# A hybrid decoder layer on one core: MLA's query norm applied in the softmax, its squares on ScalarE, and another order of the projections

## The chip, the cores and the metric

The kernel runs on one core of a Trainium2 chip. The metric is the device time of one execution in microseconds. Of a kernel, one execution is profiled; its trace gives start and length of each instruction on TensorE (PE; its weight loads are PEld), the vector engine (DVE), ScalarE (ACT), GpSimd (POOL) and the DMA queues (SP issues them).

## The reference

One decoder layer over 256 tokens, width 2048, float32. Half an FFN, then two groups of heads side by side, then half an FFN again:

```
x = x + 0.5 * swiglu(rms_norm(x, ffn1_norm), ...)           # d_ff 5632
proj = rms_norm(x, mix_norm) @ w_in
(q_a, k_cmp, v_cmp, k_sel, v_sel, k_win, v_win, g_a, c_q, c_kv, k_rope) = split(proj)
o_a = nsa_mixer(...)      # 8 sparse heads of 128: compressed, selected and window keys, gated
o_b = mla_mixer(...)      # 8 heads, below
x = x + concat(rms_norm(o_a), rms_norm(o_b)) @ w_out
x = x + 0.5 * swiglu(rms_norm(x, ffn2_norm), ...)

def mla_mixer(c_q, c_kv, k_rope, ...):
    q = (rms_norm(c_q, q_a_gain) @ w_uq).reshape(B, S, 8, 192)
    kv = (rms_norm(c_kv, kv_a_gain) @ w_ukv).reshape(B, S, 8, 256)
    k_nope, v = kv[..., :128], kv[..., 128:]
    k = concatenate([k_nope, k_rope of each head], -1)
    q = rms_norm(q, q_gain); k = rms_norm(k, k_gain)          # over 192
    q, k: the last 64 of 192 rotated by position (rope)
    s = q @ k^T * 192 ** -0.5, causal;  p = softmax(s);  o = p @ v
```

## The kernel before

Every weight is read once, as float32, and split into two parts that TensorE takes at its full rate: ScalarE casts `w_hi`, the vector engine subtracts to give `w_lo`. A product is then three matmuls (`mm3`). Weights come through three `raw` buffers on SP's queue in the order in which `weights` lists them; five split pairs may be ahead (`SPLIT`). In the middle part only as many as `SOON` allows are split at once; others wait until ScalarE and the vector engine have nothing more urgent.

All instructions are written out by a planner when the kernel is built. `go` keeps a clock per engine from rough costs. At each step it lets a finished split go on, then a side task (a generator that yields the condition it waits for), and only then the next piece of the dense stream of matmuls. The order that comes out is fixed: on the chip each engine runs its list in order and waits where an operand is late.

The middle part (`mix`) has this dense stream: the compressed keys, then tokens' projections by `TOKENS` ("0" and "1": four sparse queries each, "g": gates and MLA's query latent, 408 columns, "c": MLA's key latent, 320 columns), then by `MERGE` four up projections of queries (`q0` to `q3`, 384 columns, two heads each), four of keys and values (`k0` to `k3`, 512 columns), and the output projection in 16 pieces (`p0` to `p7` read the sparse heads, so wait for all of them, `p8` to `p15` the MLA heads).

Beside it run the heads as side tasks. A sparse head (`nsa_head`): scores into banks `ps_s`; on the vector engine bias added and maximum taken (`p_e`, `p_m`); exponential with sums on ScalarE (`p_z`); scaling on the vector engine; two "flips", transposes on TensorE into `ps_t`, each copied to `p_t` by ScalarE; the weighting of values into `ps_t`; `gather` evicts it (ScalarE `mha` and the square `sq`, vector engine `mha` and `oss`). An MLA head (`mla_head`) has one such softmax. `ps_t` has two banks in turn, which all transposes share.

An up projection's result is copied by ScalarE to a `wait` tile (four of them). For a query pair `up_q_rest` then squares it on the vector engine (`dot`, result `mss`), takes 1/sqrt (`rsqrt`: four steps on the vector engine, ten on GpSimd, scratch tiles `nw_v`, `nw_w`, `nw_t`), multiplies the 192 columns of each head by it (`mrs`), rotates the last 64 (`rope`: gain, cosine, sine, result `qr`), and turns it by transposes into `mla`. `up_k_rest` does the like for keys. The task's second number in `spawn` is its rank: rank 2 and 3 also wait until the vector engine's clock is near.

Of the kernel before, what the change touches and what calls it, by code (L numbers as in the profile page):

```python
# [7 lines left out]
F32 = mybir.dt.float32  # L8
# [28 lines left out]
TOKENS = "0g1c"  # L37
WEAVE = "abababab"

MERGE = [(m[0], int(m[1:])) for m in "q0 q1 q2 q3 k0 k1 p0 k2 p1 k3 p2 p3 p4 p5 p6 p7 p8 p9 p10 p11 p12 p13 p14 p15".split()]  # L40
PACE = 3.0

LAG, SOON = 1.0, 2
# [121 lines left out]
class _Layer:  # L165
# [637 lines left out]
    def mix(self, h, ssq, after):  # L803
# [4 lines left out]
        with self.tc.tile_pool(name="mx", bufs=1) as mx, ExitStack() as early, ExitStack() as lately:  # L808
# [19 lines left out]

            pos = const("pos", [P, 2, 32], 1)
            okc = const("okc", [P, 2])  # L830
            rot = const("rot", [P, 2, 2, 64])
            rgain = const("rgain", [P, 2, 64])
# [81 lines left out]
            self.spawn(clear())  # L914

# [188 lines left out]
            def latent_kv(p):  # L1104
# [47 lines left out]
            mla = {}  # L1152
# [37 lines left out]
            def up_q_end(i, p):  # L1190
                arrays()
                ss = brief([P, 2, 2], "mss", bufs=8)
                rs = brief([P, 2, 2], "mrs", bufs=8)
# [5 lines left out]
                self.spawn(up_q_rest(i, n, qs, ss, rs), 2)  # L1199
# [187 lines left out]
            def mla_head(hd):  # L1387
                i, j = divmod(hd, 2)
                H = hd + 8
                yield self.at(f"qT{i}", f"kT{i}", f"s{H - 1}", f"f{H - 2}")  # L1390
# [10 lines left out]
                z = brief([P, 2, 2], "p_z", bufs=2)  # L1401
# [193 lines left out]
```

## Time and profile before

| | us |
|---|---|
| three executions, median | 1822.61 (1820.01 to 1823.04) |
| the profiled execution | 1822.96 |
| its span, first to last instruction | 1821.2 |
| TensorE busy | 1800.5 |
| vector engine busy | 1457.4 |
| ScalarE busy | 992.9 |
| GpSimd busy | 45.3 |

The span is what the trace covers; 1.8 us lie around it. Busy times of engines overlap. TensorE's matmuls are pipelined, and a busy TensorE at half clock counts as busy: the granted clock has to be read beside it. The middle part lies between some 740 and 1115 us of the span.

### The profile page before, as it was taken

Reading aid. Unit: us, or ns where it says so; the run is one execution under the profiler, and the core shown is the slowest. Engines: PE = TensorE matmul, PEld = TensorE weight load, DVE = VectorE, ACT = ScalarE, POOL = GpSimd, SP = SyncE. Lnnn points to the kernel's source line nnn. Section 1 sums busy time; section 2 is a strip of 40 time slices with the busy share of each in tenths; the row PEclk is TensorE's granted clock in tenths of the full one; section 3 lists DMA queues with packets and bytes.
Section 4 is the critical chain, followed back from the end, with each engine's and each line's share of the span. In section 5 each row is a group of like instructions: output and inputs, shape, how many; then the busy total and the mean of one; then the engine's idle time right before and its main releaser. Section 6 shows DMA issues by size and latency. Waiting matters only on the chain.

```text
span 1821.2 us, 30455 instructions
## 1 busy us (share of the span) xinstructions
PE 1800.5 (99%) x12187; PEld 1645.0 (90%) x12187; DVE 1457.4 (80%) x2273; ACT 992.9 (55%) x1381; POOL 45.3 (2%) x132
## 2 busy tenths in 40 slices
PE   9999999999999999999998999999999999999999
PEld 8999999999999998888876789999999999999997
DVE  5887878979798896766778766787878989798894
ACT  6565655555555544555564545465655555555542
POOL 0000000000000000001013000000000000000000
PEclk9999999999999999999998999999999999999999
DMA  8555555555555555675233255455555655555554
GB/s 323 181 196 196 195 209 185 209 185 190 204 194 203 190 189 174 219 266 201 93 120 128 93 185 173 175 201 192 189 205 187 209 183 205 188 208 202 191 182 144
DMA packets 55950, 344.30 MB, mean 189 GB/s; under 512 B 6656, under 2 KB 8960, under 8 KB 19200
## 3 DMA queue, kind: packets, MB, share of 16 engines
q1 hardware_dynamic: 55808, 342.36, 54.0%
q8 instruction: 95, 1.56, 0.3%
q14 instruction: 47, 0.39, 0.1%
HBM read 340.24 MB, written 2.10 MB: 188 GB/s over the span
## 4 chain that ended last, share of the span: by engine, by line
PE 94%; DVE 3%; ACT 1%; DMA 1%; issue 1%; POOL 0%; SPq 0%; DVEq 0%; ACTq 0%
PE ps_u L281 47%; PE ps_m L281 19%; PE ps_acc L281 14%; PE ps_g L281 4%; PE ps_l L281 4%; PE ps_s L281 3%; DVE w_lo L141 1%; PE ps_t L281 1%; PE ps_t L296 1%; DMA raw<-in_ffn_first 0%; DVE junk L141 0%; ACT h L141 0%; DVE h L141 0%; DVE wait L141 0%; DMA raw<-in_w_cmp 0%
## 5 line engine op out<-in xcount | busy, mean ns | idle before, releaser
L141 DVE TENSOR_TENSOR w_lo<-raw,w_hi 128x1024 fp32r<-128x1024 f32 (+3 forms) x649 | 767.7, 1199 | 219.8 <-ACT w_hi L141 219.0
L141 ACT CAST w_hi<-raw 128x1024 fp32r<-128x1024 f32 (+3 forms) x649 | 660.7, 1033 | 505.0 <-PE ps_u L281 221.7
L281 PE MATMUL ps_u<-h,w_hi 128*128 128x256 f32 x4864 | 855.2, 279 | 0.0
L281 PEld LDWEIGHTS ps_u<-h,w_hi 128*128 128x128 f32 x4864 | 746.2, 188 | 6.9
L281 PE MATMUL ps_u<-h,w_lo 128*128 128x256 f32 x2432 | 679.2, 279 | 0.0
L281 PEld LDWEIGHTS ps_u<-h,w_lo 128*128 128x128 f32 x2432 | 457.1, 188 | 0.3
L281 PE MATMUL ps_m<-w_hi,act 128*128 128x512 f32 x1008 | 329.0, 396 | 0.0
L141 ACT CAST w_hi<-tsum 128x1024 fp32r<-128x1024 f32 (+1 forms) x144 | 120.6, 838 | 213.4 <-DVE tsum L141 117.9
L281 PEld LDWEIGHTS ps_m<-w_hi,act 128*128 128x128 f32 x1008 | 189.9, 188 | 43.0
L281 PE MATMUL ps_m<-w_lo,act 128*128 128x512 f32 x504 | 199.8, 396 | 0.0
L141 DVE TENSOR_TENSOR w_lo<-tsum,w_hi 128x1024 fp32r<-128x1024 f32 (+1 forms) x144 | 134.6, 953 | 33.8 <-ACT w_hi L141 33.7
L281 PE MATMUL ps_acc<-w_hi,h 128*128 128x512 f32 (+2 forms) x384 | 120.3, 381 | 0.0
L281 PEld LDWEIGHTS ps_m<-w_lo,act 128*128 128x128 f32 x504 | 94.6, 188 | 19.5
L141 DVE TENSOR_TENSOR tsum<-tsum,raw 128x512 f32<-128x512 f32 x144 | 98.5, 684 | 0.0
L281 PE MATMUL ps_l<-w_hi,act 128*128 128x512 f32 x256 | 82.6, 398 | 0.0
L281 PEld LDWEIGHTS ps_acc<-w_hi,h 128*128 128x128 f32 x384 | 71.2, 188 | 12.3 <-issue 1.6
L281 PE MATMUL ps_g<-h,w_hi 128*128 128x256 f32 x448 | 79.0, 280 | 0.2 <-DVE ff_g L141 0.2
L281 PE MATMUL ps_acc<-w_lo,h 128*128 128x512 f32 (+2 forms) x192 | 71.6, 373 | 0.0
L281 PE MATMUL ps_acc<-h,w_hi 128*128 128x256 f32 (+1 forms) x320 | 69.9, 307 | 0.8 <-ACT w_hi L141 0.8
L281 PEld LDWEIGHTS ps_g<-h,w_hi 128*128 128x128 f32 x448 | 68.2, 188 | 0.3 <-issue 0.3
L281 PE MATMUL ps_g<-h,w_lo 128*128 128x256 f32 x224 | 62.4, 279 | 0.0
L281 PEld LDWEIGHTS ps_l<-w_hi,act 128*128 128x128 f32 x256 | 48.2, 188 | 11.3
(244 smaller groups left out, 1702.9 us busy)
## 6 DMA issues: line engine op xcount, KB each, us to landing
raw<-in_ffn_gate SPq DMA_DIRECT2D x83, 1024.0 KB, 4.8
raw<-in_ffn_up SPq DMA_DIRECT2D x83, 1024.0 KB, 4.8
raw<-in_ffn_down SPq DMA_DIRECT2D x72, 1024.0 KB, 4.8
raw<-in_ffn_rest SPq DMA_DIRECT2D x32, 512.0 KB, 3.3
raw<-in_w_out SPq DMA_DIRECT2D x16, 1024.0 KB, 4.8
raw<-in_w_q SPq DMA_DIRECT2D x8, 1024.0 KB, 4.9
raw<-in_ffn_first SPq DMA_DIRECT2D x7, 768.0 KB, 8.0
raw<-in_w_cmp SPq DMA_DIRECT2D x4, 1024.0 KB, 4.8
```

What stands on the lines that cost most here:

```text
L141: r = f(*args, **kw)
L281: self.nc.tensor.matmul(out, l, r, start=start, stop=stop)
L296: self.nc.tensor.transpose(out, src, self.ident if ident is None else ident)
```

## The change

The norm of MLA's queries is no longer multiplied into them. They are rotated and turned as they come from the projection. Their squares are taken afterwards by ScalarE, 1/sqrt of the sums (`mrs`, and `mns` with the sign turned, one more step of GpSimd) is kept per pair in `qn`, and the softmax applies it: the exponential takes it as its scale, and the maximum is multiplied by it (`p_mb`), eight small steps of the vector engine. The keys keep their scaling, but ScalarE takes their squares. The gains of the rotated part are multiplied into cosine and sine once (`rots`), so a rotation has two multiplies where it had three. `rsqrt` gets scratch tiles of its own for queries and keys, two of each. Three settings of the order change as well.

```diff
-TOKENS = "0g1c"
+TOKENS = "0gc1"
-MERGE = [... "q0 q1 q2 q3 k0 k1 p0 k2 p1 k3 p2 p3 p4 p5 p6 p7 p8 ... p15".split()]
+MERGE = [... "q0 k0 q1 k1 q2 k2 q3 k3 p0 p1 p2 p3 p4 p5 p6 p7 p8 ... p15".split()]
-LAG, SOON = 1.0, 2
+LAG, SOON = 1.0, 3
+            def square(out, x, n):
+                junk = sp.tile([P, 512], F32, name="junk", tag="junk")
+                S.activation(junk[:, :n], x, AF.Square, accum_out=out)
...
+            def turning():
+                yield self.fresh(rot, rgain)
+                yield self.at("rbm")
+                for i in range(2):
+                    for m in range(2):
+                        V.tensor_mul(rots[:, i, m], rot[:, m], rgain[:, i][:, None, :].to_broadcast([P, 2, 64]))
+                self.mark("rots", rots)
...
-            def up_q_rest(i, n, qs, ss, rs):
+            def up_q_rest(i, n, qs):
                 yield self.fresh(qs)
-                for tb in range(2):
-                    for j in range(2):
-                        dot(ss[:, tb, j:j + 1], qs[:, tb, j], 192)
-                yield self.fresh(ss)
-                self.rsqrt(rs, ss, "m", 1.0, 192 * EPS)
-                yield self.fresh(rs)
                 if i:
                     yield self.at(f"qT{i - 1}")
                 qr2 = brief([P, 2, 2, 64], "qr2")
-                for tb in range(2):
-                    V.tensor_mul(qs[:, tb], qs[:, tb], rs[:, tb][:, :, None].to_broadcast([P, 2, 192]))
-                self.rope(qr2, qs[:, :, :, P:], rgain[:, 0], rot, brief, 2)
-                yield self.fresh(qs)
+                self.rope(qr2, qs[:, :, :, P:], rots[:, 0], brief, 2)
                 yield self.slot()
                 yield from up_turn(qs, qr2, i, "qT", "qr", G_MQ)
+                for tb in range(2):
+                    yield lambda: S.clk - LAG
+                    for j in range(2):
+                        square(ss[:, tb, j:j + 1], qs[:, tb, j], 192)
                 self.mark(f"left{n}")
+                yield self.fresh(ss)
+                self.rsqrt(rs, ss, f"mq{i % 2}", 1.0, 192 * EPS)
+                G.tensor_scalar(ns, rs, -1.0, None, op0=ALU.mult)
+                qn[i] = rs, ns
...
             def up_k_rest(i, n, ks, ss, rs):
-                        dot(ss[:, tb, j:j + 1], ks[:, tb, j], P)
+                        square(ss[:, tb, j:j + 1], ks[:, tb, j], P)
-                self.rsqrt(rs, ss, "m", 1.0 / 192, EPS)
+                self.rsqrt(rs, ss, f"mk{i % 2}", 1.0 / 192, EPS)
...
             def mla_head(hd):
-                    soft(e, z, m, 0, lo, n, tb, s[:, lo:lo + n], biases[8])
+                    V.tensor_tensor_reduce(out=e[:, lo:lo + n], in0=s[:, lo:lo + n], in1=biases[8][:, lo:lo + n], scale=-1.0,
+                                           scalar=3e38, op0=ALU.add, op1=ALU.min, accum_out=m[:, tb, 0:1])
+                V.tensor_mul(mb, m[:, :, 0], rs[:, :, j])
+                for tb, (lo, n) in enumerate(HALF):
+                    S.activation(e[:, lo:lo + n], e[:, lo:lo + n], AF.Exp, scale=ns[:, tb, j:j + 1], bias=mb[:, tb:tb + 1],
+                                 accum_out=z[:, tb, 0:1])
...
     def rope(...):
-        V.tensor_mul(g, src, gain[:, None, None, :].to_broadcast(sh))
-        V.tensor_mul(c, g, rot[:, 0][:, :, None, :].to_broadcast(sh))
-        V.tensor_mul(g, g, rot[:, 1][:, :, None, :].to_broadcast(sh))
+        V.tensor_mul(out, src, rot[:, 0][:, :, None, :].to_broadcast(sh))
+        V.tensor_mul(g, src, rot[:, 1][:, :, None, :].to_broadcast(sh))
```

The order on the vector engine, where a query pair of before is normed and rotated (`mss`, `mrs`: squares and norms of a pair, `wait`: the pair, `ISA` the squaring with its accumulator read). Before:

```order
L141 TENSOR_SCALAR nw_v<-mss 128x4
L141 TENSOR_SCALAR nw_w<-mss 128x4
L141 TENSOR_SCALAR mrs<-nw_v 128x4
L141 TENSOR_SCALAR mrs<-mrs 128x4
L141 TENSOR_TENSOR wait<-wait,mrs 128x384 x2
L141 TENSOR_TENSOR ro_g<-wait,rgain 128x256
L141 TENSOR_TENSOR ro_c<-ro_g,rot 128x256
L141 TENSOR_TENSOR ro_g<-ro_g,rot 128x256
L141 TENSOR_TENSOR qr_10225<-ro_c,ro_g 128x4x32 x2
L141 SCALAR_TENSOR_TENSOR mha<-ps_t,par,mha 128x256
L141 TENSOR_TENSOR oss_8985<-oss_8985,sq 128x256
L141 ISA junk,mss<-wait 128x192
```

In the changed kernel, the same step of the third query pair, with head 5's eviction and the start of head 7's scaling behind it:

```order
L141 TENSOR_SCALAR nw_v<-mss 128x4
L141 TENSOR_SCALAR nw_w<-mss 128x4
L141 TENSOR_SCALAR mrs<-nw_v 128x4
L141 TENSOR_SCALAR mrs<-mrs 128x4
L141 TENSOR_TENSOR qr_10273<-wait,rots 128x256
L141 TENSOR_TENSOR ro_g<-wait,rots 128x256
L141 TENSOR_TENSOR qr_10273<-qr_10273,ro_g 128x4x32 x2
L141 SCALAR_TENSOR_TENSOR mha<-ps_t,par,mha 128x256
L141 TENSOR_TENSOR oss_8990<-oss_8990,sq 128x256
L141 RECIPROCAL p_z<-p_z 128x4
L141 TENSOR_TENSOR p_z<-p_z,gate 128x4
L141 TENSOR_SCALAR p_e<-p_e,p_z 128x128 x2
```

The pair is only rotated; its square, its scaling and one multiply are gone from this queue, and the four short steps ahead of it belong to another pair's norm.

The order on TensorE around the scores of the last sparse heads (`nsa` holds their queries and keys, `cT` the latents that the up projections read). Before, from head 7's scores to the next flip (`p_e`):

```order
L281 MATMUL ps_s<-nsa 128x256
L281 MATMUL ps_s<-nsa 128x512
L281 MATMUL ps_t<-p_t,nsa 128x256
L281 MATMUL ps_t<-p_t,nsa 128x128
L281 MATMUL ps_t<-p_t,nsa 128x256
L281 MATMUL ps_t<-p_t,nsa 128x128
L281 MATMUL ps_t<-c_p,vcR 128x256
L296 MATMUL ps_t<-ident,p_e 128x128 x3
L281 MATMUL ps_acc<-w_hi,cT 128x384
L281 MATMUL ps_acc<-w_lo,cT 128x384
L281 MATMUL ps_acc<-w_hi,cT 128x384 x2
L281 MATMUL ps_acc<-w_lo,cT 128x384
```

In the changed kernel, from a flip of head 5 through head 7's scores to the weighting of head 5:

```order
L296 MATMUL ps_t<-ident,p_e 128x128 x6
L281 MATMUL ps_s<-nsa 128x256
L281 MATMUL ps_s<-nsa 128x512
L296 MATMUL ps_t<-ident,kr_10051 128x128 x2
L281 MATMUL ps_acc<-w_hi,cT 128x384
L281 MATMUL ps_acc<-w_lo,cT 128x384
L281 MATMUL ps_acc<-w_hi,cT 128x384
L281 MATMUL ps_t<-p_t,nsa 128x256
L281 MATMUL ps_t<-p_t,nsa 128x128
L281 MATMUL ps_t<-p_t,nsa 128x256
L281 MATMUL ps_t<-p_t,nsa 128x128
L281 MATMUL ps_t<-c_p,vcR 128x256
```

The heads 4 to 7 now stand later, among alternating up projections, with shorter runs of dense matmuls between their pieces (here three, where 18 followed before).

The order on ScalarE ahead of the first output projection, which needs a pair of the dense stream's banks that a copy `wait<-ps_acc` frees. Before, from head 7's square of its output:

```order
L141 ACTIVATE sq<-ps_t 128x256
L141 ACTIVATE mla<-ps_t,par 128x512
L141 CAST w_hi<-raw 128x1024
L141 COPY mla<-ps_t 128x256
L141 COPY wait<-ps_acc 128x256
L141 COPY mla<-ps_acc 128x256
L141 COPY wait<-ps_acc 128x256
L141 COPY mla<-ps_acc 128x256
```

In the changed kernel, from four squares of a key pair (`junk,mss<-wait`) ahead of head 7's eviction:

```order
L141 ACTIVATE junk,mss<-wait 128x128 x4
L141 ACTIVATE mha<-ps_t,par 128x256
L141 ACTIVATE sq<-ps_t 128x256
L141 ACTIVATE junk,mss<-wait 128x192 x2
L141 ACTIVATE mla<-ps_t,par 128x512
L141 CAST w_hi<-raw 128x1024
L141 ACTIVATE junk,mss<-wait 128x192 x2
L141 COPY wait<-ps_acc 128x384 x2
L141 COPY mla<-ps_t 128x256
```

Before, no square of `wait` stands on ScalarE. Now eight of them stand between the evictions and the copies that free the banks.

## Rows read from the trace of the kernel before

**Rows 1.** The page's first part: busy time, share, instructions of each engine.

```profile
PE 1800.5 (99%) x12187; PEld 1645.0 (90%) x12187; DVE 1457.4 (80%) x2273; ACT 992.9 (55%) x1381; POOL 45.3 (2%) x132
```

**Rows 2.** Stretches: busy us of PE, PEld, DVE, ACT, POOL; clock; DMA, GB/s.

```profile
864.00:917.00 53.00, 53.00 (x295) 45.09 (x294) 36.40 (x119) 27.00 (x60) 3.27 (x10) 1.00 0.30 95
917.00:947.00 30.00, 29.48 (x163) 25.17 (x162) 25.66 (x119) 21.29 (x63) 0.00 (x0) 1.00 0.32 101
947.00:967.00 20.00, 14.51 (x56) 10.82 (x57) 15.87 (x63) 9.59 (x20) 9.61 (x31) 0.83 0.27 94
967.00:996.00 29.00, 25.56 (x107) 18.55 (x105) 26.27 (x82) 13.44 (x27) 12.99 (x36) 0.88 0.58 193
996.00:1030.00 34.00, 34.00 (x168) 25.33 (x168) 21.40 (x88) 21.76 (x61) 3.11 (x14) 1.00 0.10 37
```

**Rows 3.** The same view, from head 4's scores to head 7's weighting.

```profile
916.60:956.90 40.30, 36.06 (x187) 29.90 (x185) 32.70 (x141) 27.05 (x73) 6.22 (x20) 0.96 0.37 121
```

**Rows 4.** What PE waited for, 925 to 1000: us, times, longest.

```profile
PE ps_t L296 <- DVE mha L141: 2.4, 1, 2.4
...
PE ps_t L296 <- DVE wait L141: 2.4, 2, 1.4
...
PE ps_t L296 <- DVE qr L141: 1.1, 1, 1.1
```

**Rows 5.** Timeline of DVE: start, us, operation, [idle before, releaser].

```profile
949.51 0.36 DVE L141 CUSTOM_DVE_ANT_0 junk<-wait 128x192 f32<-128x192 f32 x1
...
957.12 0.17 DVE L141 TENSOR_SCALAR nw_v<-mss 128x4 f32<-128x4 f32 x1 [2.69 <-POOL mrs L141]
957.61 1.02 DVE L141 TENSOR_TENSOR wait<-wait,mrs 128x384 f32<-128x384 f32 x2
958.67 0.42 DVE L141 TENSOR_TENSOR ro_g<-wait,rgain 128x256 f32<-128x256 f32 x1
```

**Rows 6.** DVE groups by form, 740 to 1110: busy us, mean ns, idle.

```profile
L141 DVE CUSTOM_DVE_ANT_0 junk<-wait 128x192 f32<-128x192 f32 x16 | 5.7, 356 | 0.4
...
L141 DVE CUSTOM_DVE_ANT_0 junk<-wait 128x128 f32<-128x128 f32 x16 | 4.6, 290 | 0.9
...
L141 DVE DVE_READ_ACCUMULATOR2_ANT mss<- 128x1 f32 x32 | 2.6, 82 | 0.0
...
L141 DVE TENSOR_TENSOR wait<-wait,mrs 128x384 f32<-128x384 f32 x8 | 4.1, 550 | 0.0
```

**Rows 7.** ACT groups by form, whole run, same columns.

```profile
L141 ACT CAST w_hi<-raw 128x1024 fp32r<-128x1024 f32 x608 | 629.3, 1050 | 477.7 <-PE ps_u L281 221.7 <-PE ps_acc L281 78.3 <-DVE raw L141 50.2
...
L141 ACT ACTIVATE junk<-x 128x512 f32<-128x512 f32 x24 | 15.1, 629 | 0.3
...
L141 ACT ACTIVATE sq<-ps_t 128x256 f32<-128x256 f32 x14 | 5.2, 374 | 0.0
...
L141 ACT ACTIVATION_READ_ACCUMULATOR junk<-x 128x1 f32 x24 | 4.5, 188 | 0.0
...
L141 ACT ACT_TABLE_LOAD x1 | 1.3, 1283 | 0.7 <-PEq L1586 0.7
```

**Rows 8.** Timeline of ACT: first and last row of head 6's exponentials.

```profile
926.19 0.40 ACT L141 ACTIVATE p_e<-p_e,p_m 128x128 f32<-128x128 f32 x1 [0.15 <-DVE p_m L141]
...
928.03 0.19 ACT L141 ACTIVATION_READ_ACCUMULATOR p_e<-p_e,p_m 128x1 f32 x1
```

**Rows 9.** Chain of waits, 860 to 1010: start us, us, work.

```profile
878.57 0.66 PE ps_t L296 x6
...
879.23 1.29 PE ps_s L281 x4
...
891.50 1.94 PE ps_t L281 x10
...
996.86 2.79 PE ps_acc L281 x12
...
999.97 1.89 PE ps_s L281 x8
```

More of the change, by code (lines that the diff above doesn't have):

```diff
@@ L36 @@
 NEVER = 1e9
-TOKENS = "0g1c"
+TOKENS = "0gc1"
 WEAVE = "abababab"
-MERGE = [(m[0], int(m[1:])) for m in "q0 q1 q2 q3 k0 k1 p0 k2 p1 k3 p2 p3 p4 p5 p6 p7 p8 p9 p10 p11 p12 p13 p14 p15".split()]
+MERGE = [(m[0], int(m[1:])) for m in "q0 k0 q1 k1 q2 k2 q3 k3 p0 p1 p2 p3 p4 p5 p6 p7 p8 p9 p10 p11 p12 p13 p14 p15".split()]
 PACE = 3.0
-LAG, SOON = 1.0, 2
+LAG, SOON = 1.0, 3
 FINE = (1, 3, 5)
@@ L827, in dot @@
                                        op0=ALU.mult, op1=ALU.add, accum_out=out)
+            def square(out, x, n):
+                junk = sp.tile([P, 512], F32, name="junk", tag="junk")
+                S.activation(junk[:, :n], x, AF.Square, accum_out=out)
             pos = const("pos", [P, 2, 32], 1)
             okc = const("okc", [P, 2])
-            rot = const("rot", [P, 2, 2, 64])
-            rgain = const("rgain", [P, 2, 64])
+            rot = const("rot", [P, 2, 2, 64], 1)
+            rgain = const("rgain", [P, 2, 64], 1)
+            rots = tile([P, 2, 2, 2, 64], "rots")
             fold = const("fold", [P, 64], 1)
@@ L914, in mix @@
             self.spawn(clear())
+            def turning():
[5 more added lines that the diff above has]
+                self.mark("rots", rots)
+            self.spawn(turning())
             def windows(kv):
@@ L1112, in latent_kv @@
                 self.spawn(latent(0, t, n, 0))
+                yield self.at("rots")
                 yield self.fresh(krope)
@@ L1116, in latent_kv @@
                     dot(krss[:, tb:tb + 1], krope[:, tb], 64)
-                self.rope(kr[:, :, None, :], krope[:, :, None, :], rgain[:, 1], rot, brief, 1)
+                self.rope(kr[:, :, None, :], krope[:, :, None, :], rots[:, 1], brief, 1)
                 self.mark("kr", kr, krss)
@@ L1149, in queries @@
                 return then
-            mla = {}
+            mla, qn = {}, {}
             def up_q(i):
@@ L1198, in up_q_end @@
                 self.leave(*p)
[L1199 to L1201 removed]
+                self.spawn(up_q_rest(i, n, qs), 2)
+            def up_q_rest(i, n, qs):
                 yield self.fresh(qs)
[L1203 to L1208 removed]
                 if i:
@@ L1389, in mla_head @@
                 H = hd + 8
-                yield self.at(f"qT{i}", f"kT{i}", f"s{H - 1}", f"f{H - 2}")
+                yield self.at(f"qT{i}", f"kT{i}", f"qn{i}", f"s{H - 1}", f"f{H - 2}")
                 vm, kTm, qTm, kTr, qTr = (mla[n] for n in ("v", "kT", "qT", "kr", "qr"))
@@ L1401, in mla_head @@
                 z = brief([P, 2, 2], "p_z", bufs=2)
+                rs, ns = qn[i]
+                mb = brief([P, 2], "p_mb", bufs=2)
                 for tb, (lo, n) in enumerate(HALF):
-                    soft(e, z, m, 0, lo, n, tb, s[:, lo:lo + n], biases[8])
+                    V.tensor_tensor_reduce(out=e[:, lo:lo + n], in0=s[:, lo:lo + n], in1=biases[8][:, lo:lo + n], scale=-1.0,
+                                           scalar=3e38, op0=ALU.add, op1=ALU.min, accum_out=m[:, tb, 0:1])
                 self.leave(s)
                 self.mark(f"s{H}")
+                yield self.fresh(m)
+                V.tensor_mul(mb, m[:, :, 0], rs[:, :, j])
+                yield self.fresh(mb)
+                for tb, (lo, n) in enumerate(HALF):
+                    S.activation(e[:, lo:lo + n], e[:, lo:lo + n], AF.Exp, scale=ns[:, tb, j:j + 1], bias=mb[:, tb:tb + 1],
+                                 accum_out=z[:, tb, 0:1])
                 yield self.fresh(z)
@@ L1497, in up, with rope @@
         return p
-    def rope(self, out, src, gain, rot, tile, heads):
+    def rope(self, out, src, rot, tile, heads):
         V = self.V
```

11 lines of the change are left out of this document (6 added, 5 removed).

## The prediction

> **What bounds the kernel now.** I read the totals first: TensorE is busy for 99% of the span [rows 1], so a gain can only come from where it is not. Then the stretches [rows 2]: between 864 and 917 us, and again after 996, it never stops at granted clock 1.00. In the three stretches between 917 and 996 it lacks 0.52, 5.49 and 3.44 us, together **9.45 us**. There the vector engine is busiest: 26.27 of 29 us in the last of them, against 36.40 of 53 in the first stretch. This is the stage in which the last sparse heads (4 to 7) and MLA's norms run beside the up projections.
>
> The granted clock is the second half of the loss. Its mean of 0.83 over 20 us and 0.88 over 29 us, with the two levels 1.2 and 2.4 GHz, means 20 x 0.17 x 2 + 29 x 0.12 x 2 = 13.8 us at the lower level, each stretch of it behind idle time of TensorE. If TensorE was busy there as in the two stretches on the whole (40.07 of 49 us), half of 11.3 us, or 5.6 us, was lost; if always, 6.9. I take **6.1 us**. So waits and clock together cost about **15.5 us** here, and that is the most that this change can win.
>
> What TensorE waits for is the vector engine [rows 4]: `mha` (2.4 us, the eviction that frees a bank), `wait` (2.4 us, a query or key being scaled), `qr` (1.1). The vector engine's own timeline says why [rows 5]: the squares of queries stand in its queue in front of the evictions; a norm's first step waits 2.69 us for GpSimd, whose chain still holds the shared scratch tiles; then come scaling and rotation, one behind the other.
>
> **The change part by part.** Removed from the vector engine: 16 query and 16 key squares with their accumulator reads, 5.7 + 4.6 + 2.6 = 12.9 us; the queries' scaling, 4.1 us; one multiply in each of four rotations of queries, 4 x 0.42, and a smaller one for the keys [rows 5, 6]. That is some 19 us. Added to it: four multiplies of 128 elements for `rots`, and 8 tiny ones for `mb`, bounded by the 0.29 of a square and the 0.17 of a tiny step [rows 5, 6], so 1.2 and 1.4 us. Net, **16 us** less. TensorE does the same matmuls, so none of this is a gain by itself; it only is one where TensorE waits.
>
> ScalarE gets the 32 squares. No row of before shows one so short with its accumulator read. Below, a 256-element square without the read takes 0.37; above, 512 elements take 0.63 + 0.19 [rows 7]. Four exponentials with their reads, of 128, 128, 256 and 256 elements, ran from 926.19 to 928.22 [rows 8], 0.51 each, so I take 0.4 for 128 and 0.45 for 192 elements: **13.6 us** in all (bounds 12 and 26). Its load from 917 to 996 was 44.3 of 79 us [rows 2]. No table switch is added: the whole run has one table load [rows 7], with squares and exponentials mixed already.
>
> The trace prices a query square at 0.36 + 0.08 on the vector engine and about as much on ScalarE. The Trainium skill, page "ScalarE: Activation LUTs", section "Rules for kernel authors", says to leave multiplications to VectorE. By that rule the move would give nothing, since no square gets cheaper. By the rows it pays, because the queue that TensorE waits for is the vector engine's, and ScalarE was idle for 35 of the 79 us.
>
> The scratch tiles are now separate for queries and keys and for odd and even pairs. This removes the wait of 2.69 us. A query's transposes no longer wait for its norm: square, four steps, and a GpSimd chain of ten are needed only by the exponential.
>
> The moves matter as much. The keys' latent (96 matmuls, 320 wide) goes ahead of the last four queries, and the up projections alternate, all eight ahead of the output projection. Head 4's scores so start later by about that work, near 934 instead of 917. From there to the last weighting of head 7 the changed PE order holds 4 score pairs (1.29 each), one MLA score (1.89), 4 weightings (1.94), 27 matmuls of 384 and 21 of 512 columns (2.79 for twelve of 512, in proportion for 384), and 32 transposes (0.66 for six) [rows 9]: 5.2 + 1.9 + 7.8 + 4.7 + 4.9 + 3.5 = **27.9 us**. Before, the same events spanned 40.3 us, with 36.06 of TensorE, 32.70 of the vector engine and 27.05 of ScalarE [rows 3].
>
> In that stretch the vector engine loses 12 squares (12 x 0.44 = 5.3); the latent's norm, 14 steps of two elements at 0.17 to 0.2 and some ten larger ones at 0.3, about 6 us, now lies ahead of it, while two keys' norms and scaling come in (about 3). That leaves 32.7 - 5.3 - 3 = 24.4 us. ScalarE holds four heads' exponentials (4 x 2.03), ten squares (4.1), five casts (5 x 1.05 [rows 7]), and about 24 evictions and copies (0.37 for 256 elements): some 26 us. So three engines are full to about nine tenths, each in a fixed order: **short waits stay**. Following the three orders through, these are the ones I find, each priced by what is queued ahead.
> - Weighting of head 4: its two copies `p_t` stand on ScalarE behind head 5's exponentials (2.0) and two casts (2 x 1.05). They end about 1.0 us late.
> - Second flip of head 5: the bank comes free with `mha` of head 4, which ScalarE starts after head 6's exponentials. 1.1 us.
> - First output projection: its banks come free with `wait` copies behind two pairs of squares and a cast. 0.6 us.
>
> Together **2.7 us** (bounds 1 and 5). In the rows of the last queries' projection the keys' latent norm stands ahead of `w_lo`, with almost no slack: 0.5 (0 to 3). The last queries' own chain (8 squares, GpSimd, scaling) is as long as the up projections put beside it, some 11 us: 0.5 (0 to 1.5). Behind the first output projection I find nothing over 0.5, and allow 1.0 (0 to 4). The clock: before, 9.45 us of idle cost 6.1, that is 0.65 for each us; for 4.7 us of idle in shorter pieces I take **1.7** (0 to 5). The sum is 2.7 + 0.5 + 0.5 + 1.0 + 1.7 = 6.4 us in place of 15.5. The gain is **9.1 us**: the profiled execution took 1822.96 (span 1821.2), so **1814 us**; against the median of 1822.61 that is 0.35 less again, which I leave.
>
> **Rivals.**
> - New waits on ScalarE take half the gain back. Eight blocks of four squares, 1.6 to 1.8 us each, stand in front of evictions that TensorE needs. Four of them waited for in full, 6.8 us, in place of the 1.6 that I allow: 1819. For it: the block in front of the first output projection. Against: most blocks fall where ScalarE idles.
> - ScalarE becomes the bound, and nothing is won: 44.3 + 13.6 = 58 us of work in a stage that should shrink from 79 to 70. Packed as well as the vector engine while that set the pace (67.8 of 79, 86%) it needs 67 us and does not bind; at 75% it needs 77, and the time is 1821. The rule of the Trainium skill, page "ScalarE: Activation LUTs", would end here too.
> - Slower: the four heads take as long as before, 40.3 us, because each head's own chain (score, maximum, exponential, scaling, flip, copy, weighting) sets the pace and not the load. With only 27.9 us of matmuls beside it, 12.4 us of idle follow, and 8.1 of clock: 20.5 against 15.5, so **1828**. It decides when the heads take over 37.3 us (9.4 of idle, 1.65 each). Against: before, their chains waited behind the very squares that go.
>
> **How the numbers follow.** Likeliest 0.58; half taken back 0.20; nothing won 0.12; slower 0.10. The likeliest reaches from its lower bounds (1 us lost: 1808) to about 1819. I give 1808 to 1822, which takes in the two middle rivals. A measurement of this kernel tells about 0.2%, 3.6 us, from no change: faster is the first case and two thirds of the second, 0.72; same 0.17; slower 0.11.
>
> **What would show it.** Right: TensorE's idle from head 4's scores to the last MLA head under 5 us, no single wait over 1.5, at most one or two stretches at the lower clock; `wait` and `mha` gone or small among what it waits for; the vector engine 16 us less busy, ScalarE 12 to 15 more. Squares near 0.4. Wrong: waits of TensorE put down to ScalarE (`p_t`, `wait`, `mla`) of more than 5 us, heads 4 to 7 over 37 us, or `w_lo` late in the last queries' rows.

## The result, and the profile after

The changed kernel takes **1807.38 us** (median of 6 executions, 1806.83 to 1808.15) where the kernel before takes 1822.03: ratio 0.9922, 95% interval 0.9909 to 0.9935. It is 14.6 us faster; 1814 was forecast. Its profiled execution took 1807.16 with a span of 1805.2, 16.0 less than before.

The page's first part of the changed kernel, as in [rows 1]:

```profile
PE 1790.1 (99%) x12187; PEld 1639.1 (91%) x12187; DVE 1442.2 (80%) x2208; ACT 1005.1 (56%) x1445; POOL 45.7 (3%) x136
```

The vector engine has 15.2 us less to do, ScalarE 12.2 more. The stretches of [rows 2] (the same columns), and as the last row the stretch from head 4's scores to head 7's weighting, as in [rows 3]:

```profile
864.00:917.00 53.00, 53.00 (x289) 44.62 (x288) 39.23 (x127) 28.49 (x63) 0.00 (x0) 1.00 0.40 142
917.00:947.00 30.00, 29.36 (x159) 24.05 (x157) 24.79 (x96) 26.68 (x80) 10.23 (x30) 1.00 0.54 177
947.00:967.00 20.00, 19.12 (x99) 14.66 (x98) 14.18 (x53) 14.69 (x48) 2.52 (x11) 1.00 0.25 78
967.00:996.00 29.00, 27.09 (x138) 20.79 (x136) 20.85 (x82) 24.08 (x72) 16.32 (x53) 1.00 0.27 96
996.00:1030.00 34.00, 34.00 (x162) 26.65 (x162) 22.82 (x69) 17.83 (x40) 0.00 (x0) 1.00 0.28 95
933.90:964.70 30.80, 29.46 (x146) 22.01 (x144) 24.55 (x98) 25.06 (x82) 5.65 (x21) 1.00 0.35 122
```

TensorE lacks 0.64, 0.88 and 1.91 us, together 3.43 where it was 9.45, and the granted clock is 1.00 throughout. What it waits for from 860 to 1040 us (total, times, longest), as in [rows 4]:

```profile
PE ps_acc L281 <- ACT wait L141: 1.7, 1, 1.7
PE ps_t L296 <- DVE mha L141: 0.9, 1, 0.9
PE ps_t L281 <- ACT p_t L141: 0.4, 1, 0.4
PE ps_t L296 <- ACT mla L141: 0.2, 1, 0.2
PE ps_t L296 <- ACT nsa L141: 0.2, 1, 0.2
```

No wait for a scaled query is left. The longest is one for ScalarE, ahead of the first output projection. ScalarE's timeline there, as in [rows 8], shows a cast and two squares (0.36 and 0.19 each, overlapping by 0.1) in front of the copies (`wait`) that free the bank; the output projection starts at 970.90. The cast itself began only after ScalarE had stood idle for 1.66 us, which a matmul of the dense stream ended, and the squares and copies stood behind it:

```profile
968.60 1.05 ACT L141 CAST w_hi<-raw 128x1024 fp32r<-128x1024 f32 x1 [1.66 <-PE ps_acc L281]
969.55 0.36 ACT L141 ACTIVATE junk<-wait 128x192 f32<-128x192 f32 x1
...
970.39 0.84 ACT L141 COPY wait<-ps_acc 128x384 f32<-128x384 f32 x2
```

Where did 16.0 us come from? Two groups of matmuls that the change leaves alone bracket the stage: `bsp` (the hidden layer of the compressed keys) and `mhb` (the second half of the output projection). A tile's view gives min, median and max of the durations in ns, then the first and the last start. Before:

```profile
L281 PE MATMUL ps_s<-w_hi,bsp x64: 278/279/282, 762.7 to 818.6; 128*128 128x256 f32 x64
L281 PE MATMUL ps_acc<-w_hi,mhb x128: 390/393/479, 1053.7 to 1100.7; 128*128 128x512 f32 x128
```

After:

```profile
L281 PE MATMUL ps_s<-w_hi,bsp x64: 276/279/285, 760.8 to 816.3; 128*128 128x256 f32 x64
L281 PE MATMUL ps_acc<-w_hi,mhb x128: 392/394/484, 1038.6 to 1085.8; 128*128 128x512 f32 x128
```

Between the last `bsp` and the first `mhb`, 235.1 us became 222.3: **12.8 us**. That is what idle time (9.45 - 3.43 = 6.0) and half of the 13.8 us at 1.2 GHz (6.9) give. But 2.3 us were won before the stage and 0.9 behind it (767.5 to the end of the span, then 766.6): **3.2 us outside the stage that the change is about**. Of these, 0.9 are there when the first matmul with `act` (the hidden layer of a feed-forward block) starts, at 78.3 us before and 77.4 after. The same tile's view, before and after:

```profile
L281 PE MATMUL ps_m<-w_hi,act x1008: 388/395/400, 78.3 to 1738.5; 128*128 128x512 f32 x168
L281 PE MATMUL ps_m<-w_hi,act x1008: 389/392/404, 77.4 to 1722.8; 128*128 128x512 f32 x168
```

In the runs below that leave `h` in its place this start lies anywhere from 77.0 (squares_twice) to 78.6 (norm_back), though none of them changes the work ahead of it. So up to some 1.5 us between two profiled executions can come from there alone. The rest lies in the feed-forward blocks, in the pace of the matmuls with `act`. Groups by form, before:

```profile
L281 PE MATMUL ps_m<-w_hi,act 128*128 128x512 f32 x1008 | 329.0, 396 | 0.0
L281 PE MATMUL ps_m<-w_lo,act 128*128 128x512 f32 x504 | 199.8, 396 | 0.0
```

After:

```profile
L281 PE MATMUL ps_m<-w_hi,act 128*128 128x512 f32 x1008 | 327.5, 394 | 0.0
L281 PE MATMUL ps_m<-w_lo,act 128*128 128x512 f32 x504 | 198.9, 395 | 0.0
```

From start to start (means over the trace) such a matmul of 512 columns takes 233.9 ns before and 232.5 after, which is 0.92 of a column for each period of 2.4 GHz. For 1512 of them the 1.4 ns make **2.1 us**.

### The profile page after: what moved, and what is told of

The parts are those of the page before. It is cut to its first block, busy times and chain, and to the rows that moved or that the text cites. A ratio compares the mean times of both kernels' runs of the same rounds, so it can differ in the third digit from the quotient of the medians.

```text
span 1805.2 us, 30451 instructions
## 1 busy us (share of the span) xinstructions
PE 1790.1 (99%) x12187; PEld 1639.1 (91%) x12187; DVE 1442.2 (80%) x2208; ACT 1005.1 (56%) x1445; POOL 45.7 (3%) x136
## 4 chain that ended last, share of the span: by engine, by line
PE 96%; ACT 2%; DVE 1%; DMA 1%; issue 0%; SPq 0%; DVEq 0%; ACTq 0%
PE ps_u L281 47%; PE ps_m L281 19%; PE ps_acc L281 15%; PE ps_g L281 4%; PE ps_l L281 4%; PE ps_s L281 3%; PE ps_t L281 1%; PE ps_t L296 1%; ACT w_hi L141 0%; DVE w_lo L141 0%; DMA raw<-in_ffn_first 0%; ACT junk L141 0%; ACT h L141 0%; DVE h L141 0%; ACT p_e L141 0%
## 5 line engine op out<-in xcount | busy, mean ns | idle before, releaser
L141 DVE TENSOR_TENSOR w_lo<-raw,w_hi 128x1024 fp32r<-128x1024 f32 (+4 forms) x649 | 768.5, 1200 | 220.0 <-ACT w_hi L141 219.2
L141 ACT CAST w_hi<-raw 128x1024 fp32r<-128x1024 f32 (+4 forms) x649 | 660.3, 1032 | 497.3 <-PE ps_u L281 221.2
L281 PE MATMUL ps_m<-w_hi,act 128*128 128x512 f32 x1008 | 327.5, 394 | 0.0
L281 PE MATMUL ps_m<-w_lo,act 128*128 128x512 f32 x504 | 198.9, 395 | 0.0
L281 PEld LDWEIGHTS ps_l<-w_hi,act 128*128 128x128 f32 x256 | 48.1, 188 | 11.1
```

The lines of the kernel that those rows point to most:

```text
L141: r = f(*args, **kw)
L281: self.nc.tensor.matmul(out, l, r, start=start, stop=stop)
```

## The experiments on the parts of the change

Two theories at first. A: the vector engine's load was the cause, the squares above all. B: the order did it. After the first four runs A split in two: C1, the shared scratch tiles; C2, the queries' norm ahead of their transposes.

**order_alone** is the kernel before with the new settings.

```diff
-TOKENS = "0g1c"
+TOKENS = "0gc1"
-MERGE = [... "q0 q1 q2 q3 k0 k1 p0 k2 p1 k3 p2 ..."]
+MERGE = [... "q0 k0 q1 k1 q2 k2 q3 k3 p0 p1 p2 ..."]
-LAG, SOON = 1.0, 2
+LAG, SOON = 1.0, 3
```

> The kernel before with the three settings of the changed kernel's order (keys' latent ahead of the last queries, up projections in turns, SOON 3); norm, squares and scratch tiles as before. Theory A, the gain is the vector engine's queue: the squares, the scaling and the shared scratch still stand there, so waits for it stay near the 9.4 us of before, at the lower clock too, and the time is 1816 to 1826 us. Rival B, the order does it, since it lays matmuls without a wait beside the heads' chains: at most 1811 us, with no stretch at the lower clock.

Measured 1821.69 us, ratio 0.9996 (0.9985 to 1.0007): nothing. TensorE's waits for `mha` are 6.4 us. B falls.

**norm_alone** is the changed kernel with that diff turned round.

> The changed kernel with the three settings of the order put back; norm in the softmax, squares on ScalarE and separate scratch tiles stay. Theory A, the vector engine's queue: most of the gain is there, 1808 to 1813 us, and waits for the vector engine in the stage under 5 us. Rival B, the order does it: 1817 us or more, since the last four queries' projection still ends ahead of the latent, and the heads' chains stand with too little beside them.

Measured 1808.12 us, 0.9919 (0.9902 to 0.9936): all but 0.7 us of the gain. Two waits, 0.99 us for `mha` and 1.32 for `cT`, have a stretch at the lower clock behind them. The profiled execution is the slowest of its four (1810.40). Two others had the full clock throughout and took 1806.42 and 1807.43, as little as the changed kernel, so the 0.7 us go with the clock of the other two.

**squares_on_vector** computes the squares on the vector engine at the place where ScalarE had them; the planner's clocks are kept, so the rest of the order is that of the changed kernel. The edit comes to this:

```diff
-                S.activation(junk[:, :n], x, AF.Square, accum_out=out)
+                V.eng.tensor_tensor_reduce(out=junk[:, :n], in0=x, in1=x, scale=1.0, scalar=0.0,
+                                           op0=ALU.mult, op1=ALU.add, accum_out=out)
```

> The changed kernel with its 32 squares computed by the vector engine again, at the same places of the program, the order of everything else kept; the norm still goes into the softmax. Some 13 us of work come back into the vector engine's queue. Theory A, that queue: TensorE waits for it 5 to 9 us more and loses clock, 1815 to 1822 us. Rival B, the order: the vector engine now has room (20.9 of 29 us busy from 967 to 996), 1807 to 1810 us.

Measured 1807.14 us, 0.9913 (0.9898 to 0.9928), the same as the changed kernel.

```profile
947.00:996.00 49.00, 46.72 (x237) 35.70 (x236) 41.70 (x178) 30.86 (x80) 20.64 (x66) 1.00 0.29 99
```

With 41.7 of 49 us of the vector engine busy from 947 to 996 (35.0 after the change, the third and fourth row above) TensorE's waits from 860 to 1060 sum to 2.8 us, against 3.4. The wait ahead of the first output projection is 0.8 in place of 1.7: the squares in front of its copies cost 0.9 there, and the rest is the cast, which starts only when a matmul lets it (here ScalarE is idle for 2.50 us ahead of it). So moving the squares to ScalarE won nothing in the kernel as it is now.

**squares_twice** does each square twice on ScalarE; the second writes the same sum again, and the planner's clocks leave it out.

```diff
                 S.activation(junk[:, :n], x, AF.Square, accum_out=out)
+                S.eng.activation(junk[:, :n], x, AF.Square, accum_out=out)
```

> The changed kernel with each of the 32 squares done twice by ScalarE, the order of everything else kept: some 14 us more of ScalarE's work in the stage. Theory A1, the blocks of squares mostly lie where ScalarE would idle: 1807 to 1811 us. Theory A2, ScalarE is nearly the bound after the change (24.1 of 29 us busy from 967 to 996), so that every block delays an eviction: TensorE's waits for ScalarE grow by 6 us or more, 1814 to 1822 us.

Measured 1820.85 us, 0.9985 (0.9975 to 0.9995): 13.5 us worse than the changed kernel, for 14 us more of ScalarE's time (page: 1005.1 to 1019.4). Its waits from 860 to 1060:

```profile
PE ps_acc L281 <- ACT wait L141: 2.7, 1, 2.7
PE ps_t L296 <- ACT nsa L141: 1.9, 1, 1.9
PE ps_t L296 <- DVE mhb L141: 1.6, 1, 1.6
PE ps_t L296 <- ACT c_p L141: 1.3, 1, 1.3
PE ps_t L296 <- DVE mha L141: 0.9, 1, 0.9
PE ps_t L281 <- ACT p_t L141: 0.4, 1, 0.4
```

A2's time holds: behind the first 14 us ScalarE has no room for a second. Its waits for ScalarE grew by less than A2 said, from 2.5 to 6.3 us and not by 6 or more. The larger part is the clock, which fell with the waits, to 0.83 from 917 to 947 and 0.91 from 967 to 1004: 30 x 0.17 and 37 x 0.09, together 8.4 us.

**one_scratch** is the changed kernel with one scratch set for all; **scratch_alone** the kernel before with four sets.

```diff
-                self.rsqrt(rs, ss, f"mq{i % 2}", 1.0, 192 * EPS)
+                self.rsqrt(rs, ss, "m", 1.0, 192 * EPS)
-                self.rsqrt(rs, ss, f"mk{i % 2}", 1.0 / 192, EPS)
+                self.rsqrt(rs, ss, "m", 1.0 / 192, EPS)
```

> The changed kernel with one set of scratch tiles for all the norms of queries and keys, as before; the order of all instructions is the same. Theory C1, what cost time was a norm's first step on the vector engine waiting for GpSimd to let go of the shared tiles, with the evictions (mha) queued behind it: such waits of 2 to 3 us return two or three times, with clock, and the time is 1813 to 1821 us. Theory C2, it was the scaling of the queries behind GpSimd's chain that blocked the queue, which is gone here: 1807 to 1810 us.

> The kernel before with four sets of scratch tiles for the norms of queries and keys (and seven buffers in place of eight for sums and norms, to make room); the order of all instructions is that of before. Theory C1, the shared scratch: most of the gain, 1808 to 1814 us. Theory C2, the scaling behind GpSimd's chain: waits for mha and wait stay, 1817 to 1823 us.

one_scratch: 1810.85 us, 0.994 (0.9925 to 0.9955), between the ranges of the two theories. That looks like 3.4 us for the scratch, but TensorE's waits are those of the changed kernel to the tenth (`wait` 1.7, `mha` 0.9, `p_t` 0.4). What differs is the pace in the feed-forward blocks, `ps_m` 329.0 and 199.8 us again, as before the change, for 2.1 of the 3.4 us. About 1 us more lies in the middle part of the two profiled executions, where other tiles have moved as well; its cause is open. scratch_alone: 1817.52 us, 0.9985 (0.9975 to 0.9995), with `ps_m` at 327.5 and 198.9, and waits for `mha` (2.4), `wait` (1.6) and `qr` (1.1) still there. Separate tiles move the tiles behind them; before_shifted, below, has that alone. Two programs that differ in a tile's size must not be compared without this. C1 falls: scratch_alone is no faster against before than before_shifted (0.9985 and 0.9983), so the scratch and its wait of 2.69 us [rows 5] are worth nothing that shows, in the old order or the new.

**all_but_norm** is scratch_alone with the squares on ScalarE, in the old order; **norm_back** the same in the new order.

```diff
-                        dot(ss[:, tb, j:j + 1], qs[:, tb, j], 192)
+                        square(ss[:, tb, j:j + 1], qs[:, tb, j], 192)
-                        dot(ss[:, tb, j:j + 1], ks[:, tb, j], P)
+                        square(ss[:, tb, j:j + 1], ks[:, tb, j], P)
```

> The kernel before, in its own order, with the 32 squares on ScalarE and four sets of scratch tiles (and seven buffers in place of eight for sums and norms): all of the change but the norm in the softmax, its rotation and the order. Against norm_alone (1808), which has the norm in the softmax too. Theory C1, the shared scratch: 1808 to 1812 us. Theory C2, the scaling behind GpSimd's chain: 1816 to 1823 us, with waits for the scaled queries (wait, qr) and for mha.

> The order of the changed kernel, its four scratch sets and squares on ScalarE, but the queries normed and scaled ahead of their transposes, as before (and seven buffers in place of eight for sums and norms). Theory C2, the scaling that waits for GpSimd's chain blocks the vector engine's queue and the transposes: idle of 6 to 9 us with waits for wait, qr and mha, 1812 to 1818 us. Rival B2, the up projections in turns put enough matmuls beside each pair's chain to cover it: 1807 to 1810 us.

all_but_norm 1812.88 us, 0.995 (0.9933 to 0.9967); norm_back 1811.48, 0.9942 (0.993 to 0.9955). Both lie between the theories: the norm ahead of the transposes costs 4.8 us in the old order (against norm_alone) and 4.1 in the new (against the changed kernel), with one wait for `mha` of 3.0 or 2.2 us. With it come the third multiply of the rotation and the place of the squares, ahead of the transposes; no run takes these apart from it.

**load_back** is squares_on_vector with three multiplies for each query pair that nothing reads.

```diff
+                for tb in range(2):
...
+                    V.eng.tensor_mul(extra, qs[:, tb], qs[:, tb])
...
+                V.eng.tensor_mul(extra[:, :, :P], qs[:, 0, :, :P], qs[:, 1, :, :P])
                 self.rope(qr2, qs[:, :, :, P:], rots[:, 0], brief, 2)
```

> The changed kernel with the vector engine's work of before put back without its waits: the 32 squares there again (none on ScalarE), and for each pair of queries two multiplies of 384 elements and one of 256 that nothing reads, some 6 us, in place of scaling and the third multiply of the rotation; the order of everything else kept. Theory A, the vector engine's load costs: 1812 us or more. Theories C1 and C2, only what waits in its queue costs: 1807 to 1810 us.

Measured 1810.54 us, 0.9939 (0.9924 to 0.9954): nearer to C than to A, and slightly above C's range. All 19 us of work are back on the vector engine (by their groups; the page's busy time rises from 1442.2 to 1456.6), and cost 3.2. Squares_on_vector has 13 of them at no cost. The other 6 stand ahead of the transposes, and there the new waits are (`mss` 1.4, `qr` 0.9).

**order_scratch** is scratch_alone in the new order, so norm_back with its squares on the vector engine.

> scratch_alone in the order of the changed kernel, which is norm_back with the 32 squares on the vector engine. Theory S, the squares cost where a transposition waits for the norm behind them, so with the norm ahead of the transposes their place matters: 4 to 7 us slower than norm_back (1811.5), 1815 to 1819 us. Rival: their place does not matter in this order, as it does not with the norm in the softmax (squares_on_vector, 1807.1 against 1807.4): 1810 to 1813 us.

Measured 1816.76 us, 0.9971 (0.9959 to 0.9982): 5.3 us above norm_back. The theory's range holds it. The timelines of its profiled execution (1819.08, the slowest of six) show what blocks. Vector engine:

```profile
953.17 0.28 DVE L141 CUSTOM_DVE_ANT_0 junk<-wait 128x128 f32<-128x128 f32 x1
...
954.38 1.02 DVE L141 TENSOR_TENSOR wait<-wait,mrs 128x384 f32<-128x384 f32 x2
955.44 0.42 DVE L141 TENSOR_TENSOR ro_g<-wait,rgain 128x256 f32<-128x256 f32 x1
...
957.63 1.00 DVE L141 TENSOR_SCALAR p_e<-p_e,p_z 128x128 f32<-128x128 f32 x4
958.56 0.28 DVE L141 CUSTOM_DVE_ANT_0 p_e<-ps_s,bias 128x128 f32<-128x128 f32 x1
...
961.46 0.48 DVE L141 SCALAR_TENSOR_TENSOR mha<-ps_t,par,mha 128x256 fp32r<-128x256 f32 x1 [1.72 <-ACT sq L141]
```

ScalarE's:

```profile
958.94 0.40 ACT L141 ACTIVATE p_e<-p_e,p_m 128x128 f32<-128x128 f32 x1 [4.85 <-DVE p_m L141]
...
960.71 0.45 ACT L141 ACTIVATE mha<-ps_t,par 128x256 fp32r<-128x256 f32 x1
961.06 0.36 ACT L141 ACTIVATE sq<-ps_t 128x256 f32<-128x256 f32 x1
```

And TensorE's:

```profile
953.36 1.97 PE L281 MATMUL ps_s<-nsa 128*128 128x256 f32 x4
...
962.00 0.90 PE L296 MATMUL ps_t<-ident,p_e 128*128 128x128 f32 x3 [3.10 <-DVE mha L141]
```

A head's scores are made from 953.36 to some 955.3. The vector engine takes their maximum only at 958.56. In front stand four squares of a key pair (128 elements, 953.17 to 954.4), the scaling and rotation of a query pair (384 elements, to 957.2), and the scaling of another head's exponentials. So ScalarE idles for 4.85 us, its exponentials come late, its eviction (`mha`, `sq`) behind them, the vector engine's `mha` behind that, and TensorE waits 3.10 us for a bank.

Four kernels have the same order settings, four scratch sets and the same place of `act`, and so make a square:

| us | squares on the vector engine | on ScalarE |
|---|---|---|
| norm ahead of the transposes | 1816.76 (order_scratch) | 1811.48 (norm_back) |
| norm in the softmax | 1807.14 (squares_on_vector) | 1807.38 (changed kernel) |

Leaving the norm to the softmax wins 9.6 us if the squares stay on the vector engine; moving the squares wins 5.3 only while the norm is ahead of the transposes, and 0 after. Load_back (1810.54) divides the 9.6: the same work on the vector engine, with no transpose behind the norm, costs 3.4, and the remaining 6.2, clock included, are for its order, with squares and norm ahead of the transposes.

Most of the 5.3 us reached the time by way of the clock. Over the whole span the granted clock averages 0.9965 in the executions of order_scratch and 0.9994 in those of norm_back, which is 6.4 and 1.1 us. In the two profiled executions TensorE's idle time from 860 to 1060 is 7.2 and 5.0 us, and the stretch from 952 to 977 is, in order_scratch and then in norm_back:

```profile
952.00:977.00 25.00, 20.20 (x70) 14.73 (x70) 14.58 (x63) 11.55 (x33) 5.58 (x20) 0.66 0.21 80
952.00:977.00 25.00, 21.99 (x105) 15.57 (x104) 16.59 (x63) 21.59 (x73) 5.49 (x20) 0.93 0.27 93
```

## The experiments on the place of tiles

In the built program `act` begins at byte 134944 of each partition before, at 135232 after: nine small scratch tiles stand in front of it that were not there. **before_shifted** and **after_shifted** add an unused tile of 32 bytes behind the scratch tiles; no instruction differs.

```diff
                 h, ssq = nxt["h"], nxt["ssq"]
+        self.sp.tile([P, 8], F32, name="pad")
```

> The kernel before with one more tile of 32 bytes that nothing uses at the end of its scratch pool, so that act, from which the feed-forward blocks load their stationary operand, begins at a multiple of 64 bytes, as it does after the change; no instruction differs. Theory P, the place of act costs: in runs with act 32 bytes off a multiple of 64, matmuls of 512 columns with act start every 233.9 ns, else every 232.5. Then this kernel is 2.0 to 3.0 us faster than before, 1819 to 1820 us. Rival Q, the 2.4 us outside the stage come from something else (the number of scratch tiles, or chance): no change, 1821.5 to 1822.5 us.

> The changed kernel with the same unused tile of 32 bytes, which moves act off a multiple of 64 bytes; no instruction differs. Theory P, the place: 2.0 to 3.5 us slower than the changed kernel, 1809.5 to 1811 us, with the pace of 233.9 ns back. Rival Q: 1807 to 1808 us.

before_shifted: 1818.46 us against 1821.62, 0.9983 (0.9974 to 0.9991). 32 bytes are worth 3.2 us by the medians (1.6 to 4.7 by the interval; P said 2 to 3), of which the pace makes 2.1. Its groups by form:

```profile
L281 PE MATMUL ps_m<-w_hi,act 128*128 128x512 f32 x1008 | 327.5, 394 | 0.0
L281 PE MATMUL ps_m<-w_lo,act 128*128 128x512 f32 x504 | 198.9, 395 | 0.0
```

They are those of the changed kernel to the tenth. after_shifted: 1807.8 us, 0.9923 (0.9909 to 0.9936), 0.4 above the changed kernel, where P said 2 to 3.5: `ps_m` with `w_hi` went to 328.6, with `w_lo` to 198.2. So place matters, but not by whether `act` begins at a multiple of 64.

**h_aligned** places `h`, the moving operand of 8512 matmuls, ahead of the tile `ones`:

```diff
+        h, ssq = self.new_h(), self.new_ssq()
         self.ones = self.cp.tile([P, 1], F32, name="ones")
...
-        h, ssq = self.new_h(), self.new_ssq()
```

> The changed kernel with h, the moving operand of 8512 matmuls of 256 columns and stationary operand of 576, placed ahead of ones, so that it begins at a multiple of 64 bytes and not 32 bytes off; no instruction differs. Theory P1, the rule of the place holds for a moving operand too: 116.8 ns between their starts become about 116.2, 3 to 6 us in all, 1801 to 1805 us. Theory P2, only the loads of a stationary operand feel it: 1806 to 1808 us.

Measured 1831.99 us, 1.0057 (1.0044 to 1.0069): 24.6 us slower than the changed kernel, where neither theory had a loss. TensorE's waits are the same 3.4 us, its clock 1.00. Groups by form of h_aligned, and then of the changed kernel:

```profile
L281 PE MATMUL ps_u<-h,w_hi 128*128 128x256 f32 x4864 | 878.2, 283 | 0.0
L281 PE MATMUL ps_u<-h,w_lo 128*128 128x256 f32 x2432 | 688.2, 283 | 0.0
```

```profile
L281 PE MATMUL ps_u<-h,w_hi 128*128 128x256 f32 x4864 | 855.3, 279 | 0.0
L281 PE MATMUL ps_u<-h,w_lo 128*128 128x256 f32 x2432 | 679.3, 279 | 0.0
```

**w_shifted** puts 32 unused bytes behind `h` (`ssg` twice as wide) in the changed kernel, **both_shifted** in h_aligned. **h_after_ssg** and **h_after_two** place one or two small tiles ahead of `h` in place of behind it.

```diff
-        return self.cp.tile([P, 2, NG], F32, name="ssg", tag="ssg")
+        return self.cp.tile([P, 2, 2 * NG], F32, name="ssg", tag="ssg")[:, :, :NG]
```

```diff
-        h, ssq = self.new_h(), self.new_ssq()
+        ssq = self.new_ssq()
+        self.cp.tile([P, 2], F32, name="rq", tag="rq")     # h_after_two alone
+        h = self.new_h()
```

> The changed kernel with 32 bytes that nothing uses behind h: weights, their halves and act lie 32 bytes on, h stays; no instruction differs. The distance from h to the weights' halves is then that of h_aligned (57600 bytes), h's own place that of the changed kernel. Theory D, the distance of a matmul's two operands sets its pace: as slow as h_aligned, ps_u every 119.9 ns, 1828 to 1834 us. Theory H, the place of h itself does: ps_u every 116.7 ns, 1806 to 1810 us.

> h_aligned with 32 bytes that nothing uses behind h: h begins at a multiple of 64 bytes as in h_aligned, the weights' halves lie 32 bytes on, so that their distance is 32 bytes off a multiple of 64 as in the changed kernel; no instruction differs. Theory D, the distance: ps_u every 116.7 ns, 1806 to 1810 us. Theory H, the place of h: 119.9 ns, 1828 to 1834 us.

> The changed kernel with one small tile (ssg) placed ahead of h in place of behind it: h lies 32 bytes on, the weights' halves 57536 bytes from it, all else stays; no instruction differs. Theory D1, distances that are multiples of 64 are slow (57600 was): ps_u near 119.9 ns, 1826 to 1834 us. Theory D2, the pace gets worse from 57568 towards 57600 and better away from it: 116.0 to 116.7 ns, 1800 to 1808 us.

> The changed kernel with two small tiles (ssg, rq) placed ahead of h: the weights' halves lie 57504 bytes from it; no instruction differs. Theory D1, a distance that is no multiple of 64 is fast: 116.7 to 118.4 ns (57568 and 57632 had these), 1807 to 1820 us. Theory D2, better away from 57600: 115.5 to 116.7 ns, 1797 to 1808 us.

`ps_u` from start to start is the mean over such matmuls that follow one another in the trace; distance is from `h` to the first `w_hi` tile, in bytes.

| kernel | h | w_hi | distance | ps_u, ns | us | ratio to before |
|---|---|---|---|---|---|---|
| h_after_two | 33824 | 91328 | 57504 | 120.1 | 1834.13 | 1.0067 (1.0052 to 1.0082) |
| h_after_ssg | 33792 | 91328 | 57536 | 117.8 | 1816.01 | 0.9967 (0.9955 to 0.998) |
| changed kernel | 33760 | 91328 | 57568 | 116.7 | 1807.38 | 0.9922 (0.9909 to 0.9935) |
| h_aligned | 33728 | 91328 | 57600 | 119.9 | 1831.99 | 1.0057 (1.0044 to 1.0069) |
| w_shifted | 33760 | 91360 | 57600 | 119.9 | 1831.79 | 1.005 (1.0034 to 1.0067) |
| both_shifted | 33728 | 91360 | 57632 | 118.3 | 1820.31 | 0.9988 (0.9978 to 0.9997) |

h_aligned and w_shifted have different places and one distance, and agree to 0.2 us: theory D, not H. But D's own rule, by multiples of 64, failed at once: both_shifted was put at 116.7 ns or 119.9 and came at 118.3, and its time lies in neither range. h_after_ssg (117.8, a multiple of 64) and h_after_two (120.1, none) refute that rule again as D1. Both refute D2 as well, a pace that only improves away from 57600; neither time lies in a range that was given. What the table shows is that pace goes with distance; one distance alone was tried at two places, and the rule is open. The kernel's own is the best of these five, and no version in the table beats it.

## Why the prediction was right and where it failed

**Faster was right, 1814 was not**: the profiled gain was 16.0, not 9.1, and 1807.4 lies below the range. The steps that failed are the bound and the sum of what stays:
- "The most that this change can win", 15.5 us, put everything outside the three stretches at nothing. 3.2 us came from there: 2.1 from the place of `act`, 0.9 from an earlier start, which is luck and no part of the change. I counted what each edit does to instructions, and nothing of what separate scratch tiles do to addresses. before_shifted shows that term alone.
- What stays was over-sized: 6.4 us forecast, 3.4 measured. The three waits by name were 0.4, 0.9 and 1.7, 3.0 us for 2.7. That the sum is so near is luck, since the last stood at 0.6 and the first at 1.0. The last also broke the sign "no single wait over 1.5": I priced the work ahead of the copies, and not that the cast among it has to wait for a matmul (1.66 us). The late `w_lo` (0.5) did not come; the last queries' chain (0.5) and what lies behind the first output projection (1.0) are two waits of 0.2. The clock (1.7) cost nothing.
- The clock's loss before was 6.9, not 6.1: 0.8 us.

9.1 + 3.2 + 3.0 + 0.8 is 16.1. The medians differ by 14.6, since the profiled execution of before lay 0.9 above its median and that of after 0.2 below. Without the place of tiles the gain is 1818.46 - 1807.38 = 11.1 us (before_shifted against the changed kernel) or 14.6 - 2.1 = 12.5 (by the pace), which from 1822.61 is 1811.5 or 1810.1: inside the range, whose lower end of 1 us lost had no room for an unlisted term.

**The mechanism was half right.** "The queue that TensorE waits for is the vector engine's" holds, and "the moves matter as much" does not: order_alone gave nothing, and the order is worth 0.7 us at most at the end (norm_alone). Nor was it the 16 us of load as such: squares_on_vector brings 13 of them back for nothing, and load_back all of them for 3.2. What fits all of these runs is that it counts what stands in that queue between a head's scores and their maximum. There the norm's chain was squares, scaling and three multiplies; now it is a rotation of four operations. This is read from one stretch of one trace (order_scratch); no run moves that work alone. The step "by the rows it pays", on the squares, failed: it does while a transpose waits for the norm, and the same change ended that.

The Trainium skill, page "ScalarE: Activation LUTs", section "Rules for kernel authors", leaves multiplications to VectorE, and I set it aside. The measurement has both answers: 5.3 us against the rule with the norm ahead of the transposes, nothing against it or for it (1807.14 and 1807.38) with the norm in the softmax.

**Sizes that held.** Head 4's scores were put near 934 and came at 934. The four heads' stretch took 30.8 us; 27.9 of matmuls and, of the three waits, the two that fall into it (2.1) were forecast. That this is so near is luck in part: TensorE was busy for 29.46, 1.6 more than counted, and idle for 1.3, 0.8 less. There the vector engine has 24.55 us (24.4), ScalarE 25.06 (26). ScalarE's groups by form from 860 to 1060:

```profile
L141 ACT ACTIVATE p_e<-p_e,p_m 128x256 f32<-128x256 f32 x14 | 7.0, 498 | 0.2
L141 ACT ACTIVATION_READ_ACCUMULATOR junk<-wait 128x1 f32 x32 | 6.2, 192 | 0.0
L141 ACT ACTIVATE junk<-wait 128x192 f32<-128x192 f32 x16 | 5.9, 366 | 0.3
...
L141 ACT ACTIVATE junk<-wait 128x128 f32<-128x128 f32 x16 | 5.0, 316 | 0.4
L141 ACT ACTIVATE p_e<-p_e,p_mb,mns 128x256 f32<-128x256 f32 x8 | 4.8, 599 | 0.0
```

A square with its read, less the overlap of 0.1, is 0.41 and 0.46 us; 0.4 and 0.45 were taken. Not in the sum: MLA's exponential has a second operand per partition (its scale `mns`) and takes 599 ns, where the sparse heads' takes 498, so 16 of them cost 1.6 us more. The Trainium skill, page "ScalarE: Activation LUTs", section "What ACT_TABLE_LOAD costs", states some 93 ns for each such operand; the trace agrees with 101.

**The rivals.** New waits on ScalarE did not take half the gain back: those put down to it are 1.7 + 0.4 + 0.2 + 0.2 = 2.5 us, not 6.8. Slower fell: the heads took 30.8, not 40.3. ScalarE as the bound fell too, but not by far: squares_twice ends where that rival put it (1821).

## What to carry to other kernels

Ask what a value is needed for first: a factor per row that can be applied after the product leaves the chain ahead of the matmul, and then it hardly matters which engine computes it. An engine's busy share says little; look at what stands in its queue between an operand's arrival and the step that others wait for. And where a change adds or resizes a tile, compare the pace of matmuls in a stage it does not touch before reading its gain: 32 bytes were worth 2 to 3 us here, and 24.6 in another place (h_aligned).

## What the runs showed of the hardware

A matmul's pace goes with the distance in a partition between its moving and its stationary operand: 116.7 to 120.1 ns for 256 columns at five distances 32 bytes apart, with the clock at 1.00 and no wait, and 119.9 both times at the one distance that was tried at two places.

Idle time alone does not tell the clock's loss. In norm_alone two waits, 0.99 and 1.32 us, end 1.8 us apart (946.6 and 948.4); from 947 to 957 the granted clock is 0.66. In load_back eight waits, 5.8 us together and the longest 1.4, left it at 1.00. Stretches of norm_alone and of load_back:

```profile
947.00:957.00 10.00, 8.63 (x33) 6.60 (x32) 5.84 (x8) 6.82 (x15) 0.00 (x0) 0.66 0.71 247
```

```profile
925.00:947.00 22.00, 20.10 (x108) 15.43 (x106) 20.89 (x86) 14.95 (x38) 6.18 (x19) 1.00 0.45 147
947.00:996.00 49.00, 45.08 (x227) 34.34 (x228) 43.93 (x188) 29.83 (x82) 20.54 (x65) 1.00 0.26 92
```

Nor is it the same in each execution of one kernel: the four of norm_alone have a mean clock of 1.000, 1.000, 0.999 and 0.998, at 1806.4, 1807.4, 1808.8 and 1810.4 us. So the 0.65 us of clock for each us of idle, taken from one execution of before, does not carry over: after the change it was 0, and in order_scratch 25 x 0.34 = 8.5 us stand behind 7.2 of idle, 1.2 for each.
